# Stick-breaking rows by chunks from the last keys on, with only beta in a 4 KB slot

## The chip, the core and the metric

The kernel runs on one core of a Trainium2 chip. The core has a matrix engine (TensorE; in the profile PE for its matmuls and PEld for its weight loads), a vector engine (VectorE, DVE), an engine for functions such as the sigmoid (ScalarE, ACT), a general engine (GpSimd, POOL) and a queue that issues DMAs (SyncE, SP). Each takes its instructions strictly in the order that was fixed when the program was built, and stands when the next one has to wait for another engine. Operands lie in SBUF (128 partitions), matmul results in the banks of PSUM.

The metric is the device time of one execution in microseconds (us), lower being better. It is given as the median of several executions.

## What is computed

The reference is a trunk of two equal layers on 1024 tokens of width 1024. A combined projection of the stream feeds four parallel branches (latent attention "MLA", stick-breaking attention, forgetting attention "fox", attention to a memory of 256 tokens), each of 4 heads of width 64. The branches are gated and merged, projected, added to the stream and normalised. The branch that matters here:

```python
def _stick_breaking_attention(q, k, v):
    """A[t,s] = sigmoid(z[t,s]) * prod_{s<j<t} (1 - sigmoid(z[t,j])), s < t."""
    ...
    z = jnp.einsum('bqhd,bkhd->bhqk', qb, kb, preferred_element_type=jnp.float32)
    strict = jnp.arange(kend)[None, :] < (start + jnp.arange(Q_BLOCK))[:, None]
    log_keep = jnp.where(strict, jax.nn.log_sigmoid(-z), 0.0)
    ...
    a = jnp.where(strict, jnp.exp(z + incl), 0.0).astype(v.dtype)
    return jnp.einsum('bhqk,bkhd->bqhd', a, vb)
```

`incl` is the sum of `log_keep` from key s to the end of the row. So the weight of key s is beta(s) = sigmoid(z(s)), times the product of 1 - beta over all later keys that the query sees. Queries are taken in blocks of 128, and a block of queries sees the keys up to its own end.

## The kernel before

All matmuls run in a split form: an operand is held as a high and a low part, so a projection is three passes (lines 245 to 247). In each layer the branches follow one another: fox pair 0, fox pair 1, stick-breaking pair 0 and 1 (`run(units(sb[0], "sb"), ...)`, lines 840 and 845), then memory and MLA. A "pair" is two of the four heads.

A `Unit` is one head and two blocks of 128 queries ("rows" below). Its number `qg` from 0 to 3 tells how many keys its rows see: `qg` 3 has rows of 896 and 1024 keys, 2 of 640 and 768, 1 of 384 and 512, 0 of 128 and 256. The units of a head come in the order 3, 0, 2, 1 (`Q_ORDER`). Rows of more than 512 keys ("wide" rows, those of `qg` 2 and 3) take two chunks of scores, since a chunk fills one PSUM bank of 512 values: in both layers there are 64 stick-breaking rows, 32 of them wide.

`Unit.scores` (line 358) makes the rows of a unit. For stick-breaking, per chunk: two matmuls (lines 353 and 354) put the scores in a PSUM bank; ScalarE writes 1 - beta = sigmoid(-z) to `kt` and beta = sigmoid(z) to `bt` (lines 400 and 401, recorded under line 125, the helper `tfn`); at the row's last chunk POOL sets the masked part of the last 128 columns of `bt` to zero (line 403). After all chunks of the row:

```python
dve.tensor_tensor_scan(kt[:, ::-1], kt[:, ::-1], unseen[:, S - w:][:, ::-1], 1.0, ALU.mult, ALU.max)
dve.tensor_tensor(bt[:, :w - 1], bt[:, :w - 1], kt[:, 1:], ALU.mult)
```

The scan (line 416) runs from the last key back and leaves in `kt` the running product; its second operand `unseen` is 1 where the query doesn't see the key, which holds the product at 1 there. The product (line 417) takes for each key the running product of the key behind it.

`Unit.values` (line 433) then turns a row's `bt` by 128 x 128 transposes on TensorE into `pt` (line 442). `split_evac` (lines 143 to 149) copies it to `ph` on ScalarE (145) and takes the rest to `pl` on VectorE (146), and `product` (line 465) multiplies both with the values into `y` (line 472); `add_heads` (lines 460 and 461) adds up the halves. The products of a chunk are issued `LAG` = 2 chunks later.

`run` (line 510) interleaves: while the scores of one unit are made, the values of the unit `AHEAD` = 2 before it are worked through, and between the steps TensorE gets pieces of a "filler", the projections of the next pair (`pair_qkv`) or, in the second half, of `cq` and the merge input. The filler's weights come by DMA on the SP queue (line 221) and are split on POOL (lines 154 and 157); for `cq`, POOL also squares and sums (lines 749 to 753).

Storage: tiles of up to 512 float32 columns come from a pool of 64 slots of 2 KB per partition (`U`, pool `up`), wider ones from a pool of 7 slots of 4 KB (`W`, pool `wp`). Narrow rows take both `bt` and `kt` from the first pool, wide rows both from the second. A slot can be written again when the last reader of its tile is done; the framework adds the waits. It also fixes the order of the instructions on each engine: it goes by the order of the program and by when it reckons an instruction to be ready, so the order on an engine isn't just that of the text.

Of the kernel before, what the change touches and what calls it, by code (L numbers as in the profile page):

```python
# [10 lines left out]
F32 = mybir.dt.float32  # L11
F32R = mybir.dt.float32r
I32 = mybir.dt.int32
AF = mybir.ActivationFunctionType
ALU = mybir.AluOpType
# [6 lines left out]
S = 1024  # L22
# [15 lines left out]
HALF = 512  # L38
# [27 lines left out]
def decoder_trunk(ctx: ExitStack, tc: tile.TileContext, x, x_t, mem_t, positions, w_a, w_s, mla_q_norm, mla_w_qb,  # L66
# [3 lines left out]
    act, dve, pool, pe = nc.scalar, nc.vector, nc.gpsimd, nc.tensor  # L70
# [15 lines left out]
    def nm(s):  # L86
        uid[0] += 1
        return f"{s}_{uid[0]}"

    def U(s, dt=F32R):  # L90
        return up.tile([P, HALF], dt, tag="U", name=nm(s))

    def W(s, w=S):
        if w <= HALF:
            return U(s, F32)[:, :w]
        return wp.tile([P, S], F32, tag="W", name=nm(s))[:, :w]
# [4 lines left out]
    def SM(s, n=1):  # L101
        return sp.tile([P, 16], F32, tag="sm", name=nm(s))[:, :n]

    def PJ(s="pj"):
        return psj.tile([P, HALF], F32, tag="pj", name=nm(s))

    def PT(s="pt"):
        return pst.tile([P, HALF], F32, tag="pt", name=nm(s))

    def PS(s="sc"):  # L110
        return psj.tile([P, HALF], F32, tag="pj", name=nm(s))
# [8 lines left out]
    def after(later, earlier):  # L120
        tc.add_manual_dep(later.ins, earlier.ins.name,
                          mybir.DependencyInfo(mybir.DependencyClass.NoSync, mybir.DependencyReason.DATA), reason="table")

    def tfn(*args, **kw):
        i = act.activation(*args, **kw)  # L125
        if table_load[0] is not None:
            after(i, table_load[0])
        table_users.append(i)
# [39 lines left out]
    unseen = cp.tile([P, S], mybir.dt.bfloat16, name="unseen")  # L168
# [9 lines left out]
    ps = psy.tile([P, HALF], F32, tag="y", name="warm")  # L178
# [158 lines left out]
    class Unit:  # L337
# [20 lines left out]
        def scores(self):  # L358
            op, h = self.op, self.head
            if self.kind == "mem":  # L360
                ps = PS()
                for i in range(2):
                    self.qk(ps[:, i * MEM:(i + 1) * MEM], i, op["k"][h], 0, MEM)
                yield
                v3 = ps.rearrange("p (i k) -> p i k", i=2)
                mx = SM("mx", 2)
                dve.tensor_reduce(mx, v3, AX.X, ALU.max, negate=True)
                p = W("p", HALF)
                sm = SM("sm", 2)
                for i in range(2):  # L370
                    tfn(p[:, i * MEM:(i + 1) * MEM], ps[:, i * MEM:(i + 1) * MEM], AF.Exp,
                        bias=mx[:, i:i + 1], accum_out=sm[:, i:i + 1])
                dve.reciprocal(sm, sm)
                for i in range(2):
                    pool.tensor_scalar(p[:, i * MEM:(i + 1) * MEM], p[:, i * MEM:(i + 1) * MEM], sm[:, i:i + 1], 1.0,
                                       ALU.mult, ALU.mult)
                    self.p.append(p[:, i * MEM:(i + 1) * MEM])
                return
            for i in range(2):
                qb = 2 * self.qg + i  # L380
                w = (qb + 1) * P
                if self.kind == "sb":
                    bt, kt = W("bt", w), W("kt", w)
                else:
                    p = W("p", w)
                    bias = None
                    mx, sm = SM("mx", 2), SM("sm")
                if self.kind == "fox":
                    ckb, c_nat, hg = self.aux()
                    pool.tensor_scalar(p, ckb[:, :w], -1.0, c_nat[:, hg, qb:qb + 1], ALU.mult, ALU.add)  # L390
                    pool.affine_select(p[:, w - P:], p[:, w - P:], [[-1, P]], ALU.is_ge, -BIG, base=0, channel_multiplier=1)
                    bias = p
                for c0 in range(0, w, HALF):
                    n = min(HALF, w - c0)
                    ps = PS()[:, :n]
                    c = slice(c0, c0 + n)
                    self.qk(ps, i, op["k"][h][c0 // HALF][:, :n], c0, n)
                    yield
                    if self.kind == "sb":
                        tfn(kt[:, c], ps, AF.Sigmoid, scale=-1.0)  # L400
                        tfn(bt[:, c], ps, AF.Sigmoid)
                        if c0 + n == w:
                            pool.affine_select(bt[:, w - P:], bt[:, w - P:], [[-1, P]], ALU.is_gt, 0.0, base=0, channel_multiplier=1)  # L403
                    else:
                        if bias is not None:
                            b = bias[:, c]
                        elif c0 + n == w:
                            b = mask[:, HALF - n:]
                        else:
                            b = mask[:, 0:1].broadcast_to((P, n))  # L410
                        dve.tensor_tensor_reduce(out=p[:, c], in0=ps, in1=b, scale=-1.0,  # L411
                                                 scalar=mx[:, 0:1] if c0 else 3.0e38, op0=ALU.add, op1=ALU.min,
                                                 accum_out=mx[:, 1:2] if c0 else mx[:, 0:1])
                if self.kind == "sb":

                    dve.tensor_tensor_scan(kt[:, ::-1], kt[:, ::-1], unseen[:, S - w:][:, ::-1], 1.0, ALU.mult, ALU.max)
                    dve.tensor_tensor(bt[:, :w - 1], bt[:, :w - 1], kt[:, 1:], ALU.mult)
                    self.p.append(bt)
                    continue
                mx = mx[:, 1:2] if w > HALF else mx[:, 0:1]  # L420
                tfn(p, p, AF.Exp, bias=mx, scale=-1.0, accum_out=sm)
                dve.reciprocal(sm, sm)  # L422
                pool.tensor_scalar(p, p, sm, 1.0, ALU.mult, ALU.mult)  # L423
                self.p.append(p)
# [192 lines left out]
    for layer in range(DEPTH):  # L617
# [12 lines left out]
        for b in range(NB):  # L630
            if b == 4:
                drain(late_x.pop()())
            ps = PJ("pA")
# [25 lines left out]
        ps = PT("cum")  # L659
# [10 lines left out]
        ps = PT("cT")  # L670
# [53 lines left out]
        sb = [{}, {}]  # L724
# [469 lines left out]
        for col in range(2):  # L1194
# [5 lines left out]
            for t in range(NB):  # L1200
# [3 lines left out]
                ps = PJ("po")  # L1204
# [78 lines left out]
```

## Time and profile before

| | us |
|---|---|
| median of 3 runs | 1596.25 (1595.80 to 1597.51) |
| the profiled execution | 1594.06 |
| its span, first to last instruction | 1592.3 |
| mean granted TensorE clock | 0.998 |

The profile is of one execution, a little faster than the median of the others. Its span is shorter than the time of that execution by what lies before the first and after the last instruction. The groups of instructions that the change touches, by shape (engine, operation, out<-in, shapes, count; then busy time in all, mean duration in ns, and the idle time of the engine before them with what ended it):

```profile
L125 ACT ACTIVATE kt<-sc 128x512 f32<-128x512 f32 x48 | 29.4, 618 | 12.8 <-PE sc L354 12.6
L125 ACT ACTIVATE bt<-sc 128x512 f32<-128x512 f32 x48 | 29.1, 614 | 16.7 <-DVE bt L417 16.7
```

```profile
L416 DVE TENSOR_TENSOR_SCAN kt<-kt,unseen 128x896 f32<-128x896 f32 x8 | 18.3, 2291 | 0.1
L416 DVE TENSOR_TENSOR_SCAN kt<-kt,unseen 128x768 f32<-128x768 f32 x8 | 14.0, 1747 | 0.0
L417 DVE TENSOR_TENSOR bt<-bt,kt 128x895 f32<-128x895 f32 x8 | 9.6, 1194 | 0.0
L417 DVE TENSOR_TENSOR bt<-bt,kt 128x767 f32<-128x767 f32 x8 | 7.7, 967 | 0.5
```

A row of the first kind reads: 48 sigmoids of 128 x 512 take 29.4 us in all and 618 ns each, and ScalarE stood 12.8 us in front of them, 12.6 of which ended with a score matmul of line 354. In rows of a timeline the first number is the start, the second the duration. An engine that is idle costs nothing unless another one waits for it in the end.

### The profile page before, as it was taken

How to read it: one execution, taken by the hardware profiler on the slowest of the kernel's cores; microseconds unless marked ns; L12 is line 12 of the kernel's file. 1: busy time of each engine (PE TensorE's matmuls, PEld its weight loads, DVE VectorE, ACT ScalarE, POOL GpSimd, SP SyncE). 2: the span in 40 equal slices, each digit the busy share in tenths (PEclk: the TensorE clock that was granted, in tenths of full speed). 3: DMA queues.
4: the chain of work that ended last, by engine and by line, in shares of the span. 5: the costliest groups of instructions: out<-in, count | busy, mean ns of one | idle time of the engine just before them, and what ended most of it. 6: DMA issues, size and time to landing. Idle time of an engine off the chain costs nothing.

```text
span 1592.3 us, 24853 instructions
## 1 busy us (share of the span) xinstructions
PE 1559.3 (98%) x8454; PEld 1328.6 (83%) x8454; DVE 1027.2 (65%) x2047; ACT 737.7 (46%) x1628; POOL 810.3 (51%) x967
## 2 busy tenths in 40 slices
PE   9999999999999999999999999999999999999997
PEld 8888878888887888888898888788888878888886
DVE  6455588844417788882863566888444277888738
ACT  4354565534425666440423456565444256564301
POOL 5765535765544243671636654267645443446611
PEclk9999999999999999999999999999999999999999
DMA  5311112132233212252312221121422232212413
GB/s 183 113 57 54 52 35 64 54 121 59 80 108 106 70 38 60 79 172 80 116 61 87 60 62 50 30 64 58 122 61 77 101 110 70 64 39 81 149 47 119
DMA packets 86062, 127.93 MB, mean 80 GB/s; under 512 B 13424, under 2 KB 38832, under 8 KB 85936
## 3 DMA queue, kind: packets, MB, share of 16 engines
q1 hardware_dynamic: 85936, 126.34, 25.5%
q8 instruction: 67, 1.10, 0.3%
q14 instruction: 59, 0.48, 0.1%
HBM read 89.57 MB, written 19.96 MB: 69 GB/s over the span
## 4 chain that ended last, share of the span: by engine, by line
PE 83%; DVE 7%; POOL 3%; issue 3%; ACT 2%; DMA 2%; SPq 0%; DVEq 0%; ACTq 0%; POOLq 0%
PE pj L245 12%; PE pj L246 12%; PE pj L247 12%; PE y L472 6%; PE pt L442 6%; PE sc L353 3%; PE pb L245 3%; PE sc L354 3%; PE pb L246 3%; PE pb L247 3%; PE po L245 3%; PE po L247 3%; PE po L246 3%; PE pg L245 1%; PE pg L247 1%
## 5 line engine op out<-in xcount | busy, mean ns | idle before, releaser
L245 PE MATMUL pj<-xTh,wh 128*128 128x512 f32 x832 | 330.3, 397 | 0.0
L247 PE MATMUL pj<-xTh,wl 128*128 128x512 f32 x832 | 326.6, 392 | 0.0
L246 PE MATMUL pj<-xTl,wh 128*128 128x512 f32 x832 | 325.9, 392 | 0.0
L157 POOL TENSOR_TENSOR wl<-wr,wh 128x512 fp32r<-128x512 f32 x168 | 226.6, 1350 | 9.6
L154 POOL TENSOR_SCALAR wh<-wr 128x512 fp32r<-128x512 f32 x168 | 121.9, 726 | 212.9 <-PE pj L246 118.1
L146 DVE TENSOR_TENSOR pl<-pt,ph 128x384 fp32r<-128x384 f32 (+1 forms) x272 | 171.1, 637 | 90.9 <-ACT ph L145 89.0
L145 ACT CAST ph<-pt 128x384 fp32r<-128x384 f32 (+1 forms) x272 | 148.7, 552 | 141.2 <-PE pt L442 137.7
L247 PEld LDWEIGHTS pj<-xTh,wl 128*128 128x128 f32 x832 | 156.4, 188 | 31.3
L423 POOL TENSOR_SCALAR p<-p,sm 128x896 f32<-128x896 f32 (+7 forms) x128 | 102.4, 802 | 152.7 <-DVE sm L422 151.8
L245 PEld LDWEIGHTS pj<-xTh,wh 128*128 128x128 f32 x832 | 156.5, 188 | 26.6 <-DVE mx L411 1.2
L246 PEld LDWEIGHTS pj<-xTl,wh 128*128 128x128 f32 x832 | 156.5, 188 | 25.7
L125 ACT ACTIVATE p<-p,mx 128x896 f32<-128x896 f32 (+7 forms) x128 | 99.6, 778 | 65.0 <-DVE mx L411 56.3
L472 PE MATMUL y<-pl,v 128*128 128x256 f32 (+1 forms) x544 | 123.8, 305 | 0.0
L125 ACT ACTIVATE mg<-pg 128x512 f32<-128x512 f32 x128 | 76.4, 597 | 90.8 <-PE pg L247 54.4
L472 PE MATMUL y<-ph,v 128*128 128x256 f32 (+1 forms) x544 | 113.0, 285 | 0.2
L442 PE MATMUL pt<-ident_r,p 128*128 128x128 f32 x704 | 110.8, 273 | 1.5 <-DVE pl L146 1.4
L245 PE MATMUL pb<-ybh,wh 128*128 128x512 f32 x256 | 102.8, 402 | 4.7 <-ACT ybh L148 2.0
L472 PEld LDWEIGHTS y<-ph,v 128*128 128x128 f32 x544 | 92.8, 189 | 12.2 <-issue 0.9
L246 PE MATMUL pb<-ybl,wh 128*128 128x512 f32 x256 | 100.5, 392 | 0.1
L247 PE MATMUL pb<-ybh,wl 128*128 128x512 f32 x256 | 100.1, 391 | 0.0
L403 POOL TENSOR_SCALAR_AFFINE_SELECT bt<-bt 128x128 f32<-128x128 f32 x64 | 53.5, 841 | 90.4 <-ACT bt L125 85.4
L442 PEld LDWEIGHTS pt<-ident_r,p 128*128 128x128 f32 x704 | 84.7, 140 | 16.1 <-DVE pl L146 2.3
(277 smaller groups left out, 3626.6 us busy)
## 6 DMA issues: line engine op xcount, KB each, us to landing
wr<-in_w_s_dram SPq DMA_DIRECT2D x168, 256.0 KB, 2.6
s<-opA SPq DMA_DIRECT2D x128, 64.0 KB, 2.0
s<-opB SPq DMA_DIRECT2D x128, 64.0 KB, 2.0
wr<-in_w_out_dram SPq DMA_DIRECT2D x32, 256.0 KB, 2.6
xr<-in_x_t_dram SPq DMA_DIRECT2D x16, 256.0 KB, 5.6
ckb<-c_d SPq DMA_DIRECT2D x8, 512.0 KB, 4.3
y_d<-y SPq DMA_DIRECT2D x16, 256.0 KB, 2.2
y<-y_d SPq DMA_DIRECT2D x16, 256.0 KB, 3.5
```

Source lines behind the costliest of these rows:

```text
L125: i = act.activation(*args, **kw)
L145: act.copy(h, src)
L146: return dve.tensor_tensor(l, src, f(h), ALU.subtract)
L154: i = pool.tensor_scalar(h, src, 1.0, 1.0, ALU.mult, ALU.mult)
L157: pool.tensor_tensor(l, src, f(h), ALU.subtract)
L245: pe.matmul(ps, ah, bh, start=k == 0, stop=False)
L246: pe.matmul(ps, ah, bl, start=False, stop=False)
L247: pe.matmul(ps, al, bh, start=False, stop=k == nk - 1)
L403: pool.affine_select(bt[:, w - P:], bt[:, w - P:], [[-1, P]], ALU.is_gt, 0.0, base=0, channel_multiplier=1)
L423: pool.tensor_scalar(p, p, sm, 1.0, ALU.mult, ALU.mult)
L442: pe.transpose(pt[:, c:c + P], self.p[i][:, b * P:(b + 1) * P], ident)
L472: pe.matmul(u.y[:, q0 * P:256], u.op["v"][b][:, u.head, :], src[:, s * 256 + q0 * P:s * 256 + 256], start=j == 0 and n == 0, stop=j == n_c ...
```

## The change

Only the stick-breaking part of `Unit.scores` changes. A row's `kt` is no longer one tile of the row's width: each chunk has its own `kt` of at most 512 columns, from the 2 KB slots. The chunks of a row are made from the last keys to the first. The scan and the product come chunk by chunk, as soon as the chunk's sigmoids are issued. The second chunk's scan starts from `later`, the first column of the `kt` before it, and the last column of a chunk's `bt`, which needs the running product of the chunk behind it, is multiplied by `later` in an operation of its own. `bt` stays one tile of the row's width. Rows of one chunk have the same operations as before. The other kinds of units keep their order of chunks.

```diff
-                    bt, kt = W("bt", w), W("kt", w)
+                    bt, later = W("bt", w), None
...
-                for c0 in range(0, w, HALF):
+                starts = list(range(0, w, HALF))
+                for c0 in reversed(starts) if self.kind == "sb" else starts:
...
                     if self.kind == "sb":
-                        tfn(kt[:, c], ps, AF.Sigmoid, scale=-1.0)
+
+
+                        kt = U("kt", F32)[:, :n]
+                        tfn(kt, ps, AF.Sigmoid, scale=-1.0)
                         tfn(bt[:, c], ps, AF.Sigmoid)
                         if c0 + n == w:
                             pool.affine_select(bt[:, w - P:], bt[:, w - P:], [[-1, P]], ALU.is_gt, 0.0, base=0, channel_multiplier=1)
+                        dve.tensor_tensor_scan(kt[:, ::-1], kt[:, ::-1], unseen[:, S - w:][:, c][:, ::-1],
+                                               1.0 if later is None else later, ALU.mult, ALU.max)
+                        if later is not None:
+                            dve.tensor_tensor(bt[:, c0 + n - 1:c0 + n], bt[:, c0 + n - 1:c0 + n], later, ALU.mult)
+                        dve.tensor_tensor(bt[:, c0:c0 + n - 1], bt[:, c0:c0 + n - 1], kt[:, 1:], ALU.mult)
+                        later = kt[:, 0:1]
...
                 if self.kind == "sb":
-
-                    dve.tensor_tensor_scan(kt[:, ::-1], kt[:, ::-1], unseen[:, S - w:][:, ::-1], 1.0, ALU.mult, ALU.max)
-                    dve.tensor_tensor(bt[:, :w - 1], bt[:, :w - 1], kt[:, 1:], ALU.mult)
                     self.p.append(bt)
```

## The prediction

> **What bounds the kernel now.** I read the page first, then the busy time of each engine by stretch, then the waits inside the stick-breaking stretches, and last the instructions one by one at the places where TensorE stood.
>
> ```profile
> span 1592.3 us, 24853 instructions
> PE 1559.3 (98%) x8454; PEld 1328.6 (83%) x8454; DVE 1027.2 (65%) x2047; ACT 737.7 (46%) x1628; POOL 810.3 (51%) x967
> PE 83%; DVE 7%; POOL 3%; issue 3%; ACT 2%; DMA 2%; SPq 0%; DVEq 0%; ACTq 0%; POOLq 0%
> ```
>
> TensorE is busy for 98% of the span and is 83% of the chain that ended last. The change adds and removes no matmul, so it can only act on the 1592.3 - 1559.3 = 33.0 us in which PE stands, and it touches only the two stick-breaking stretches, at 184 to 330 us and again at 978 to 1122 us. The columns below are the stretch, its length, and the busy time of PE, PEld, DVE, ACT and POOL.
>
> ```profile
> core 0: us, PE busy (x) PEld busy (x) DVE busy (x) ACT busy (x) POOL busy (x), PEclk, DMA share, GB/s
> 80.00:184.00 104.00, 102.76 (x589) 88.32 (x589) 58.21 (x165) 55.83 (x121) 63.72 (x96) 1.00 0.19 55
> 184.00:260.00 76.00, 71.99 (x406) 61.07 (x406) 63.19 (x79) 44.96 (x105) 31.56 (x31) 1.00 0.14 41
> 260.00:330.00 70.00, 69.13 (x390) 59.57 (x389) 55.91 (x69) 39.29 (x86) 45.01 (x40) 1.00 0.24 76
> ```
>
> The forgetting-attention stretch (80 to 184 us) loses 1.2 us of PE. The stick-breaking one (184 to 330 us) loses 4.01 + 0.87 = 4.9 us, with VectorE busy for 119.1 of 146 us against 58.2 of 104. So the ceiling of the gain is 4.9 us a layer, 9.8 us in all, or 0.6%.
>
> Who waits for whom there (total, times, longest). The first row is of the whole span, the rest are of 180 to 332 us:
>
> ```profile
> ACT bt L125 <- DVE bt L417: 16.7, 8, 2.4
> ...
> PE sc L353 <- ACT bt L125: 2.8, 3, 2.0
> PE pt L442 <- DVE pl L146: 1.9, 3, 0.9
> ...
> DVE bt L417 <- POOL bt L403: 2.2, 3, 0.9
> ...
> ACT bt L125 <- DVE bt L417: 8.4, 4, 2.4
> ```
>
> The sigmoid that writes `bt` reads only PSUM, so nothing of its data comes from L417. It waits for storage: L417 is the last reader of an earlier row's `kt`, whose 4 KB slot the new `bt` takes. By the code, rows of two wide units are in flight (4 `bt`) while the next wide unit makes two more `bt` and two `kt`: 8 for 7 slots.
>
> This is the longest such place, in order of time (start, duration, engine; in brackets the idle time before and what ended it):
>
> ```profile
> 218.82 1.09 ACT L125 ACTIVATE kt<-sc 128x512 f32<-128x512 f32 x2
> ...
> 219.07 4.28 DVE L416 TENSOR_TENSOR_SCAN kt<-kt,unseen 128x896 f32<-128x896 f32 x2
> ...
> 221.97 0.58 ACT L145 CAST ph<-pt 128x512 fp32r<-128x512 f32 x1 [2.06 <-PE pt L442]
> ...
> 223.28 1.43 DVE L417 TENSOR_TENSOR bt<-bt,kt 128x895 f32<-128x895 f32 x1
> ...
> 224.74 0.69 DVE L146 TENSOR_TENSOR pl<-pt,ph 128x512 fp32r<-128x512 f32 x1
> 224.80 1.08 ACT L125 ACTIVATE bt<-sc 128x512 f32<-128x512 f32 x2 [2.25 <-DVE bt L417]
> 225.45 0.39 PE L353 MATMUL sc<-opB,opB 128*128 128x256 f32 x1 [2.01 <-ACT bt L125]
> ...
> 226.05 0.49 PE L472 MATMUL y<-pl,v 128*128 128x256 f32 x2
> ```
>
> ACT waits 2.25 us until the multiplication of the 896 row ends at 224.71. The score banks in PSUM stay full meanwhile, and PE waits 2.01 us for one. I call this place A; it stands once in each layer.
>
> **The change part by part.** *TensorE, ACT, DMA.* Each wide row keeps its two score chunks with the short one now first: same matmuls, same 192 sigmoids of the same sizes, no DMA added or moved past another (the SP queue's head loads and weight loads stay behind the same steps). Cost 0.
>
> *Slots.* `kt` leaves the 4 KB slots, so at most 6 of 7 are asked for and the 16.7 us of ACT waits go. Of PE's time this is worth 2.01 us at A. What is late next there is `pl`. Without its wait PE reaches the product at 226.05 - 2.01 = 224.04, and in the present VectorE order `pl` ends at 224.74 + 0.69 = 225.43: then 1.39 us of the wait would stay and 0.62 be gained. But `ph` is ready at 221.97 + 0.58 = 222.55, and `pl` comes late only because two whole scans (4.28 us) and a product stand ahead of it. In pieces of at most 512 no VectorE operation there is longer than the 1.22 us of the 512 scan below, so `pl` can start by 223.77, end by 224.46 and keep PE for 0.42. I take 2.01 - 0.42 = 1.6 us, since the planner orders by readiness; the ends are 0.62 and 2.01. The other three ACT waits of a layer cost PE at most 2.8 - 2.01 = 0.8 us; I take 0.
>
> Here a page of the Trainium skill speaks on both sides. "Perfetto Trace Analysis", section Optimizing Scalar/DVE Operations, says that grouping into larger operations helps throughput where the engine is saturated, and that breaking instructions up may let work end sooner where it is not saturated but makes bubbles elsewhere. By its first half A would gain 0.62 or less, by its second half 1.6; no run so far shows which holds.
>
> *VectorE pays* by one more scan, one more product and a one-column product for each of the 32 wide rows (columns: busy us, mean ns, idle before):
>
> ```profile
> L416 DVE TENSOR_TENSOR_SCAN kt<-kt,unseen 128x1024 f32<-128x1024 f32 x8 | 20.4, 2552 | 2.1 <-ACT kt L125 2.1
> ...
> L422 DVE RECIPROCAL sm<-sm 128x1 f32<-128x1 f32 x128 | 20.2, 159 | 32.3 <-ACT p L125 31.1
> ...
> L416 DVE TENSOR_TENSOR_SCAN kt<-kt,unseen 128x640 f32<-128x640 f32 x8 | 12.8, 1602 | 1.8 <-ACT kt L125 1.8
> L417 DVE TENSOR_TENSOR bt<-bt,kt 128x1023 f32<-128x1023 f32 x8 | 11.9, 1487 | 3.0 <-POOL bt L403 3.0
> ...
> L416 DVE TENSOR_TENSOR_SCAN kt<-kt,unseen 128x512 f32<-128x512 f32 x8 | 9.8, 1222 | 0.1
> ...
> L417 DVE TENSOR_TENSOR bt<-bt,kt 128x511 f32<-128x511 f32 x8 | 8.9, 1107 | 1.8 <-POOL bt L403 1.4
> L417 DVE TENSOR_TENSOR bt<-bt,kt 128x639 f32<-128x639 f32 x8 | 8.7, 1094 | 0.7
> ...
> L416 DVE TENSOR_TENSOR_SCAN kt<-kt,unseen 128x128 f32<-128x128 f32 x8 | 4.0, 504 | 0.1
> ...
> L417 DVE TENSOR_TENSOR bt<-bt,kt 128x127 f32<-128x127 f32 x8 | 2.7, 339 | 0.5
> ```
>
> A 1024 row: scans 2 x 1222 - 2552 = -108 ns, products 2 x 1107 - 1487 = +727 ns. A 640 row: 1222 + 504 - 1602 = +124 and 1107 + 339 - 1094 = +352 ns. The one-column product is not in this trace; the nearest row is the one-column reciprocal, 159 ns. So a wide row costs 0.64 to 0.78 us more; at 0.7 that is 22 us in all, 11 us a layer. What hides it:
>
> ```profile
> 198.70:228.40 29.70, 26.52 (x148) 22.32 (x147) 28.02 (x36) 18.48 (x40) 11.41 (x13) 1.00 0.16 49
> 228.40:233.10 4.70, 4.70 (x30) 4.11 (x29) 0.04 (x2) 0.60 (x2) 0.00 (x0) 1.00 0.06 16
> 233.10:260.00 26.90, 26.07 (x152) 22.07 (x151) 25.38 (x32) 18.27 (x44) 13.79 (x12) 1.00 0.12 35
> ```
>
> VectorE has no air around A (28.02 of 29.70). The four wide rows there add 2.8 us and then run into 4.70 us in which VectorE does nothing: covered. The next stretch has four wide rows again, 2.8 us, and only 1.5 us of air, so VectorE ends it 1.3 us later. Two units of rows stand between a row and its transposes, which should absorb that; I charge 0.3 us a layer, the ends being 0 and, if all eight rows reached PE, 5.6.
>
> *The added wait.* The masking on POOL (L403) now stands in front of the product of the last chunk, with the first chunk's scan and the next `pl` queued behind that product on VectorE, and PE behind `pl`. Before, a whole row's scan covered it and 3 of 32 rows of a layer still waited, 2.2 us. This is the second place where PE stands, B:
>
> ```profile
> 288.79 3.36 DVE L416 TENSOR_TENSOR_SCAN kt<-kt,unseen 128x1024 f32<-128x1024 f32 x1
> ...
> 289.96 3.02 POOL L752 TENSOR_TENSOR q<-cq 128x512 f32<-128x512 f32 x1
> ...
> 292.94 0.29 POOL L403 TENSOR_SCALAR_AFFINE_SELECT bt<-bt 128x128 f32<-128x128 f32 x1
> ...
> 293.26 2.29 DVE L417 TENSOR_TENSOR bt<-bt,kt 128x1023 f32<-128x1023 f32 x1 [0.67 <-POOL bt L403]
> 295.48 1.14 DVE L146 TENSOR_TENSOR pl<-pt,ph 128x384 fp32r<-128x384 f32 x2
> ...
> 296.08 0.66 PE L442 MATMUL pt<-ident_r,bt 128*128 128x128 f32 x4 [0.87 <-DVE pl L146]
> ```
>
> POOL's square ends 0.83 us after the scan that ran beside it, the mask comes behind it, the product behind the mask, `pl` behind the product, and PE waits 0.87 us. With scans of at most 1.22 us the square should end earlier and `pl` find an earlier turn: I take +0.6 us a layer. The ends are +0.87 and -1.5 (if behind the mask there stand a 512 scan, a one-column product and two 511 products, 1.22 + 0.16 + 2 x 1.11 = 3.6 us, in place of 2.29, and 0.2 of slack goes too). The Trainium skill, "SBUF — State Buffer", section Who interferes with whom, says that a VectorE operation with two SBUF inputs and a POOL operation that reads SBUF exclude each other for the whole instruction, whichever started first. By that rule half-length scans would shorten POOL's wait, but more VectorE instructions would mean more collisions. The sum needs neither.
>
> *Sum:* per layer 1.6 + 0.6 - 0.3 = 1.9 us, 3.8 us in all: 1594.06 to about 1590.3 in the profiled execution, whose span is 1592.3. The median of the three runs shown is 2.2 us above that execution, so 1596.25 - 3.8 = 1592.5. A measurement of this kernel tells about 0.2%, 3.2 us, from no change.
>
> **The rivals.**
>
> *The wait is only passed on.* `pl` keeps its turn behind the scans and products, A gives 0.62 us, B gives 0, the charge stays: 2 x (0.62 - 0.3) = 0.6 us, so 1595.6. For it: around A VectorE is busy 28.02 of 29.70 us, and work is only added. Against it: the pieces open more turns.
>
> *VectorE becomes the bound.* It decides from the point at which the added work of a stretch is more than the air behind it. The eight wide rows of 198.7 to 260 us then cost 8 x 0.7 = 5.6 us of PE a layer, less 1.6 of A: +8 us, 1604.3. For it: 25.38 of 26.90 us. Against it: 4.70 us of air after A, and the two units of lead.
>
> *The 2 KB slots run short.* By my count of the code about 60 of the 64 are held here (32 of them the split stream, then q, k, v of two pairs, finished outputs, narrow rows), and two wide rows at once ask for 4 more. If they are short, the ACT wait only changes its pool and PE's 2.8 us a layer stay or grow: with VectorE's charge doubled to 0.6 and B at -1.5, 2 x 2.1 = +4.2 us, 1600.5. Against it: `vT`, `v` and the new q and k find slots in this trace without a listed wait. This is also the case in which the change does not do what it says.
>
> **How the numbers follow.** Forecast 0.55, of which 0.44 is a gain over 0.2% and 0.11 one within it; passed on 0.24, all within 0.2%; VectorE bound 0.15 and slots 0.06, both slower. Faster 0.44, same 0.35, slower 0.21. Low end: all of A (2.01), of B (0.87) and the 0.8 of the other waits, with 0.9 us a layer of short waits besides, is 9.2 us, 1587. High end: the slots' case and part of VectorE's, 1602; beyond it are 0.05 below and 0.10 above.
>
> **What would show it.** Right: no ACT `bt` wait on a VectorE product; PE's wait at the 256 row after the wide unit falls from 2.01 to under 0.6; VectorE's busy time in the two stretches grows by some 22 us; `pl` starts within 1.3 us of `ph` there. Wrong: the same PE time reappearing as "pt" or "y" waiting for `pl` (passed on), VectorE stretches without air longer than now and PE losing over 4.9 us a layer (bound), or `kt` sigmoids waiting for TensorE or VectorE readers of other tiles (slots). A different order of instructions throughout would make the sum wrong as a whole.

## The result, and the profile after

| | before | after |
|---|---|---|
| median, us | 1596.32 | 1609.15 |
| runs, lowest to highest, us | 1595.80 to 1597.51 | 1605.72 to 1610.48 |
| ratio of the runs | | 1.0078, 95% interval 1.0062 to 1.0094 |
| profiled execution, us | 1594.06 | 1610.48 |
| its span, us | 1592.3 | 1608.8 |

The change makes the kernel 0.8% slower; the forecast was 0.2% faster, and the time lies above the range. The ratios, here and below, come from the single runs and are not the quotients of the medians shown; the two differ by up to 0.1%. The page of the kernel after (span, busy time of the engines, chain):

```profile
span 1608.8 us, 24966 instructions
...
PE 1565.7 (97%) x8454; PEld 1332.6 (83%) x8454; DVE 1053.3 (65%) x2143; ACT 739.9 (46%) x1628; POOL 788.0 (49%) x967
...
PE 87%; DVE 7%; ACT 2%; DMA 1%; issue 1%; POOL 1%; SPq 0%; DVEq 0%; ACTq 0%; POOLq 0%
```

TensorE runs the same 8454 matmuls. VectorE is busy for 26.1 us more. The chain gives VectorE 7% before and after, so it does not show where the time went. The stretches do (length, busy PE, PEld, DVE, ACT, POOL, granted clock):

```profile
80.00:184.00 104.00, 102.76 (x590) 88.36 (x589) 58.22 (x165) 55.90 (x122) 63.77 (x96) 1.00 0.19 55
184.00:260.00 76.00, 71.27 (x389) 60.06 (x388) 63.30 (x101) 42.11 (x96) 23.35 (x29) 0.96 0.14 39
260.00:330.00 70.00, 64.71 (x366) 55.01 (x365) 63.25 (x89) 38.87 (x86) 41.09 (x40) 1.00 0.18 55
...
228.40:233.10 4.70, 3.29 (x18) 2.48 (x16) 4.60 (x6) 0.00 (x0) 3.06 (x2) 1.00 0.17 38
```

Up to 184 us nothing has changed. In the stick-breaking stretch TensorE now stands 4.73 + 5.29 = 10.0 us, against 4.9 before, and from 184 to 330 us it starts 755 matmuls where before it started 796. The last row is the 4.70 us in which VectorE had been idle before: it is now busy for 4.60 of them. The second layer repeats it; these are the sums for its stretch (978 to 1122 us), first before, then after:

```profile
sum 144.00, PE 139.10 PEld 119.03 DVE 118.66 ACT 81.76 POOL 76.04; mean PE 69.55 PEld 59.51 DVE 59.33 ACT 40.88 POOL 38.02
```

```profile
sum 144.00, PE 133.76 PEld 113.54 DVE 124.44 ACT 80.86 POOL 62.18; mean PE 66.88 PEld 56.77 DVE 62.22 ACT 40.43 POOL 31.09
```

TensorE stands 10.2 us there, 4.9 before. What it waits for in the kernel after, 180 to 345 us (total, times, longest):

```profile
PE pt L449 <- DVE pl L146: 6.7, 6, 2.2
PE sc L353 <- DVE v L312: 1.7, 2, 0.8
PE sc L353 <- ACT bt L125: 0.5, 1, 0.5
```

The wait that the change was to remove is gone: `bt` cost TensorE 2.8 us, and costs 0.5. But the wait for `pl` has grown from 1.9 to 6.7 us in this layer, and to 7.2 in the other. The wait for `v` is new; it comes at 193 and 263 us, where the two pairs start. The groups of instructions show that the sigmoids no longer wait, and how long VectorE's pieces take (columns as before: count, busy us, mean ns, idle before):

```profile
L125 ACT ACTIVATE bt<-sc 128x512 f32<-128x512 f32 x48 | 29.3, 610 | 0.0
...
L408 DVE TENSOR_TENSOR_SCAN kt<-kt,kt,unseen 128x512 f32<-128x512 f32 x32 | 44.7, 1395 | 0.1
L412 DVE TENSOR_TENSOR bt<-bt,kt 128x511 f32<-128x511 f32 x48 | 44.3, 924 | 1.7 <-POOL bt L407 0.7
L408 DVE TENSOR_TENSOR_SCAN kt<-kt,unseen 128x512 f32<-128x512 f32 x16 | 23.3, 1459 | 0.1
L411 DVE TENSOR_TENSOR bt<-bt,kt 128x1 f32<-128x1 f32 x32 | 8.2, 257 | 0.0
```

ScalarE's 16.7 us in front of the `bt` sigmoids are 0.0. The 512 scan, at 1222 ns in its row before, takes 1395 to 1459 ns, and the one-column product 257 ns where I had taken 159. Half of these products take 136 ns or less; single ones take up to 1185.

Place B in order of time, the second of the places where TensorE stands:

```profile
296.47 1.53 DVE L412 TENSOR_TENSOR bt<-bt,kt 128x511 f32<-128x511 f32 x1
...
297.41 1.49 POOL L759 TENSOR_TENSOR q<-cq 128x512 f32<-128x512 f32 x1
...
297.93 2.06 DVE L408 TENSOR_TENSOR_SCAN kt<-kt,unseen 128x512 f32<-128x512 f32 x1
297.94 0.58 ACT L145 CAST ph<-pt 128x512 fp32r<-128x512 f32 x1 [2.08 <-PE pt L449]
...
298.98 2.06 POOL L760 TENSOR_TENSOR sq<-sq,q 128x512 f32<-128x512 f32 x1
...
299.90 0.53 DVE L146 TENSOR_TENSOR pl<-pt,ph 128x384 fp32r<-128x384 f32 x1
...
300.49 0.66 PE L449 MATMUL pt<-ident_r,bt 128*128 128x128 f32 x4 [2.17 <-DVE pl L146]
```

A piece of a scan, 2.06 us long beside POOL's two operations, is put in front of `pl`, though `ph` was ready at 298.52. TensorE waits 2.17 us, where it had waited 0.87. The shorter pieces didn't give `pl` an earlier turn.

A second difference lies at the start of the stretch, on ScalarE. Before, the first `kt` follows the sigmoid's table load at once:

```profile
182.79 1.28 ACT L136 ACT_TABLE_LOAD   x1
184.09 0.60 ACT L125 ACTIVATE kt<-sc 128x512 f32<-128x512 f32 x1
```

After:

```profile
182.65 1.28 ACT L136 ACT_TABLE_LOAD   x1
...
189.95 0.48 ACT L145 CAST ph<-pt 128x384 fp32r<-128x384 f32 x1 [5.04 <-PE pt L449]
...
190.58 0.65 ACT L310 CAST v<-vtp 128x256 fp32r<-128x256 f32 x2
...
192.13 0.65 ACT L310 CAST v<-vtp 128x256 fp32r<-128x256 f32 x2 [0.52 <-PE vtp L306]
192.67 0.51 ACT L125 ACTIVATE kt<-sc 128x384 f32<-128x384 f32 x1
```

The first `kt` sigmoid now comes at 192.67 us, 8.6 us later, behind the four `v` tiles of its own pair, which no data joins to it. As I read the program, a tile of the 2 KB pool is first written no earlier than the tiles of this pool that the program makes before it. `kt` of a wide row is now such a tile, and the pair's `v` is made ahead of it. Before, the first `kt` that had a 2 KB slot, that of the narrow row of 128 keys, stood right behind `v` as well:

```profile
197.31 0.65 ACT L310 CAST v<-vtp 128x256 fp32r<-128x256 f32 x2 [4.44 <-PE vtp L306]
197.84 0.30 ACT L125 ACTIVATE kt<-sc 128x128 f32<-128x128 f32 x1
```

### The profile page after: what moved, and what is told of

Its sections match the earlier page's. It is cut to its first block, busy times and chain, and to the rows that moved or that the text cites. A ratio compares the mean times of both kernels' runs of the same rounds, so it can differ in the third digit from the quotient of the medians.

```text
span 1608.8 us, 24966 instructions
## 1 busy us (share of the span) xinstructions
PE 1565.7 (97%) x8454; PEld 1332.6 (83%) x8454; DVE 1053.3 (65%) x2143; ACT 739.9 (46%) x1628; POOL 788.0 (49%) x967
## 4 chain that ended last, share of the span: by engine, by line
PE 87%; DVE 7%; ACT 2%; DMA 1%; issue 1%; POOL 1%; SPq 0%; DVEq 0%; ACTq 0%; POOLq 0%
PE pj L245 12%; PE pj L246 12%; PE pj L247 11%; PE y L479 7%; PE pt L449 6%; PE pb L245 4%; PE pb L246 4%; PE pb L247 4%; PE sc L353 3%; PE sc L354 3%; PE po L246 3%; PE po L247 3%; PE po L245 3%; DVE kt L408 2%; PE pg L245 2%; PE pg L247 2%
## 5 line engine op out<-in xcount | busy, mean ns | idle before, releaser
L479 PEld LDWEIGHTS y<-ph,v 128*128 128x128 f32 x544 | 94.0, 189 | 13.9 <-ACT ph L145 1.6
L407 POOL TENSOR_SCALAR_AFFINE_SELECT bt<-bt 128x128 f32<-128x128 f32 x64 | 36.0, 564 | 125.2 <-ACT bt L125 122.6
```

What stands on the lines that cost most here:

```text
L479: pe.matmul(u.y[:, q0 * P:256], u.op["v"][b][:, u.head, :], src[:, s * 256 + q0 * P:s * 256 + 256], start=j == 0 and n == 0, stop=j == n_c ...
```

## The experiments

Three parts of the change were in question, and each was tried alone, undone, or given room: the cut operations on VectorE, the 2 KB slots for `kt`, and the order of the chunks. All ratios are to the kernel before, run on the same chip, with 95% intervals.

**One more 4 KB slot, before otherwise unchanged.** This takes away the wait that the change was aimed at, and nothing else.

```diff
-    up = ctx.enter_context(tc.tile_pool(name="up", bufs=64))
-    wp = ctx.enter_context(tc.tile_pool(name="wp", bufs=7))
+    up = ctx.enter_context(tc.tile_pool(name="up", bufs=62))
+    wp = ctx.enter_context(tc.tile_pool(name="wp", bufs=8))
```

> Before, with 8 in place of 7 slots of 4 KB, and 62 in place of 64 of 2 KB to pay for it; nothing else. It takes the storage wait away alone. Theory P (the 2 KB pool's order is what costs) and theory V (VectorE's added operations cost): the 2.01 us wait of PE at place A goes, no ACT wait of bt on L417 is left, and the time falls by 2 to 6 us, to 1590 to 1594. If the wait was covered anyway: within 3 us of 1596. If 62 slots are too few: slower.

Measured: 1587.7 us against 1594.56, ratio 0.9953 (0.9940 to 0.9966). The `bt` group of this kernel:

```profile
L125 ACT ACTIVATE bt<-sc 128x512 f32<-128x512 f32 x48 | 29.7, 618 | 0.0
```

and its waits of TensorE for the same stretch:

```profile
PE pt L442 <- DVE pl L146: 1.2, 2, 0.7
...
PE sc L353 <- ACT bt L125: 0.4, 1, 0.4
```

So the wait was a wait for a slot, as argued, and without it `pl` is not late either: 1.2 us against 1.9. It is worth 6.9 us, more than I had expected and twice the 3.2 that I gave place A. The two 2 KB slots it takes cost nothing, which a control shows:

```diff
-    up = ctx.enter_context(tc.tile_pool(name="up", bufs=64))
+    up = ctx.enter_context(tc.tile_pool(name="up", bufs=62))
```

> Before, with 62 in place of 64 slots of 2 KB; the control of the run with 8 slots of 4 KB. If the 2 KB pool has two slots to spare: within 3 us of before. If not: slower, and the run with 8 slots has to be read against this one.

Measured: 1595.13 against 1595.33, 1.0001 (0.9992 to 1.0011).

**The cut operations alone.** Before, with scan, one-column product and product cut in two at the end of the row; scores in the old order, `kt` in its 4 KB slot.

```diff
-                    dve.tensor_tensor_scan(kt[:, ::-1], kt[:, ::-1], unseen[:, S - w:][:, ::-1], 1.0, ALU.mult, ALU.max)
-                    dve.tensor_tensor(bt[:, :w - 1], bt[:, :w - 1], kt[:, 1:], ALU.mult)
+                    later = None
+                    for c0 in reversed(range(0, w, HALF)):
+                        n = min(HALF, w - c0)
+                        c = slice(c0, c0 + n)
+                        dve.tensor_tensor_scan(kt[:, c][:, ::-1], kt[:, c][:, ::-1], unseen[:, S - w:][:, c][:, ::-1],
+                                               1.0 if later is None else later, ALU.mult, ALU.max)
+                        if later is not None:
+                            dve.tensor_tensor(bt[:, c0 + n - 1:c0 + n], bt[:, c0 + n - 1:c0 + n], later, ALU.mult)
+                        dve.tensor_tensor(bt[:, c0:c0 + n - 1], bt[:, c0:c0 + n - 1], kt[:, c][:, 1:], ALU.mult)
+                        later = kt[:, c0:c0 + 1]
```

> Before, with the scan and the product of a wide row cut into chunks as in the changed kernel, but with kt still in a 4 KB slot, the scores in the old order, and both cut operations after the whole row. Theory V (VectorE's added operations make the loss): VectorE busy some 20 us more, and most of the loss is here, 1604 to 1610. Theory P (order of the 2 KB pool) and theory R (the reversed order of chunks): within 4 us of before, 1593 to 1600.

Measured: 1604.97, 1.0059 (1.0047 to 1.0072). Cutting alone costs 9.4 us of the 1594.56, though in this kernel mostly not by way of `pl`. TensorE's longest wait, once in each layer, is for a row's own last operations (line 423 is the one-column product there); for `pl` it waits 1.3 us, not more than before:

```profile
PE pt L450 <- DVE bt L423: 4.3, 1, 4.3
```

**The order alone.** Before, with only the chunks reversed.

```diff
-                for c0 in range(0, w, HALF):
+                starts = list(range(0, w, HALF))
+                for c0 in reversed(starts) if self.kind == "sb" else starts:
```

> Before, with only the order of the two score chunks of a wide row reversed; whole scans, kt in a 4 KB slot. Theory R (the order makes the loss, since the planner then orders everything else differently): 1603 to 1610. Theories P and V: within 4 us of before.

Measured: 1589.55, 0.9961 (0.9948 to 0.9974). The reversal is no harm, but a gain, which was not expected. The `bt` group says where from:

```profile
L125 ACT ACTIVATE bt<-sc 128x512 f32<-128x512 f32 x48 | 29.2, 613 | 5.4 <-DVE bt L418 5.4
```

16.7 us of waiting for a slot have become 5.4 with the same 7 slots. If this is the same wait as the first experiment's, the two gains should not add up. The reversal above, and one more slot:

```diff
-    up = ctx.enter_context(tc.tile_pool(name="up", bufs=64))
-    wp = ctx.enter_context(tc.tile_pool(name="wp", bufs=7))
+    up = ctx.enter_context(tc.tile_pool(name="up", bufs=62))
+    wp = ctx.enter_context(tc.tile_pool(name="wp", bufs=8))
```

> Before, with the reversed order of chunks and 8 slots of 4 KB (62 of 2 KB), whole scans. If the two gains are the same wait removed in two ways: 1586 to 1590, as with either alone. If they are of different waits: 1580 to 1585.

Measured: 1588.38 against 1595.4, 0.9953 (0.9936 to 0.9970): no more than the slot alone.

**The change with `kt` back in a 4 KB slot.**

```diff
-                    bt, later = W("bt", w), None
+                    bt, kw, later = W("bt", w), W("kt", w), None
...
-                        kt = U("kt", F32)[:, :n]
+                        kt = kw[:, c]
```

> The changed kernel in everything but storage: kt of a wide row is one tile in a 4 KB slot again, whose chunks are scanned one by one in the new order. Theory P: the first sigmoids come at about 184 us again in place of 192.7, and most of the loss goes, 1594 to 1602. Theory V or R: the loss stays, 1606 to 1612.

Measured: 1597.89, 1.0016 (1.0007 to 1.0025). This is the reversal's kernel plus the cuts: 0.9961 to 1.0016, so here they cost 0.55%. And it is 0.6% faster than the whole change, so the place of `kt` costs too. With eight 4 KB slots as well, no shortage is left, and only the operations differ from the kernel with reversed order and eight slots. The edit above, and:

```diff
-    up = ctx.enter_context(tc.tile_pool(name="up", bufs=64))
-    wp = ctx.enter_context(tc.tile_pool(name="wp", bufs=7))
+    up = ctx.enter_context(tc.tile_pool(name="up", bufs=62))
+    wp = ctx.enter_context(tc.tile_pool(name="wp", bufs=8))
```

> The changed kernel with kt of wide rows in 4 KB slots of which there are 8 (62 of 2 KB): order, cut operations and enough slots, without the 2 KB pool. Theory V (the cut operations cost by themselves): 6 to 12 us above the run that has the reversed order and whole scans, 1593 to 1599. If the cut operations cost only because slots run short: within 3 us of that run.

Measured: 1600.61 against 1595.4, 1.0032 (1.0021 to 1.0043). Against its twin without cuts that is 12.2 us. The same stretch of time in both, first without cuts, then with them:

```profile
280.00:300.00 20.00, 20.00 (x115) 17.27 (x114) 16.91 (x19) 9.70 (x22) 15.79 (x14) 1.00 0.21 60
```

```profile
280.00:300.00 20.00, 17.77 (x92) 15.42 (x91) 18.05 (x20) 8.10 (x17) 13.03 (x11) 0.91 0.19 53
```

and inside them, with cuts, in order of time:

```profile
288.49 2.31 DVE L408 TENSOR_TENSOR_SCAN kt<-kt,unseen 128x512 f32<-128x512 f32 x1
...
290.73 3.00 DVE L412 TENSOR_TENSOR bt<-bt,kt 128x383 f32<-128x383 f32 x2
...
293.75 1.16 DVE L146 TENSOR_TENSOR pl<-pt,ph 128x512 fp32r<-128x512 f32 x2
...
294.50 0.90 PE L449 MATMUL pt<-ident_r,bt 128*128 128x128 f32 x3 [2.23 <-DVE pl L146]
```

A scan and two products, 5.3 us, run in front of `pl`. With whole operations TensorE does not stand there at all.

**Which of the cuts.** The reversed kernel with eight slots, with the scan cut, chunk by chunk, and the product left whole.

```diff
+                        dve.tensor_tensor_scan(kt[:, ::-1], kt[:, ::-1], unseen[:, S - w:][:, c][:, ::-1],
+                                               1.0 if later is None else later, ALU.mult, ALU.max)
+                        later = kt[:, 0:1]
...
-                    dve.tensor_tensor_scan(kt[:, ::-1], kt[:, ::-1], unseen[:, S - w:][:, ::-1], 1.0, ALU.mult, ALU.max)
-                    dve.tensor_tensor(bt[:, :w - 1], bt[:, :w - 1], kt[:, 1:], ALU.mult)
+                    dve.tensor_tensor(bt[:, :w - 1], bt[:, :w - 1], kw[:, 1:], ALU.mult)
```

> Reversed order, 8 slots of 4 KB, the scan cut by chunks as they come, but the product whole, at the row's end: one more operation for each wide row in place of three. With whole operations this is 1588, with all three 1600.6. Theory V by time (what counts is VectorE's busy time, some 5 of the 18 us): 1589 to 1593. Theory V by number (each further operation is a turn more for pl to wait for): 1591 to 1597, a third of the way. If cutting the scan is what costs: 1598 to 1602.

Measured: 1597.95 against 1595.7, 1.0013 (1.0004 to 1.0022). From 0.9953 that is 0.60%, 9.6 us, of the 0.79% that all the cuts cost: the scan's cut, which I had priced at about nothing, makes most of the loss. One row of each kernel, first the whole scans, then the cut ones:

```profile
L417 DVE TENSOR_TENSOR_SCAN kt<-kt,unseen 128x1024 f32<-128x1024 f32 x8 | 20.8, 2604 | 2.1 <-ACT kt L125 2.1
```

```profile
L408 DVE TENSOR_TENSOR_SCAN kt<-kt,unseen 128x512 f32<-128x512 f32 x48 | 69.0, 1442 | 2.4 <-ACT kt L125 1.1
```

Two halves take 2 x 1442 = 2884 ns instead of 2604. Over all widths the scans take 110.5 us instead of 96.6. Of these 48 pieces, 23 have no POOL operation on tensors beside them and take 1.27 us on average; the other 25 take 1.61 us. Among those 25, the 12 that run beside an operation of POOL on two tensors (`TENSOR_TENSOR`) take 1.92 us, the other 13 take 1.32.

**The turn in the pool.** First, the change with a pool of its own for the wide rows' `kt`: three 2 KB slots, taken from the common ones.

```diff
-    up = ctx.enter_context(tc.tile_pool(name="up", bufs=64))
+    up = ctx.enter_context(tc.tile_pool(name="up", bufs=61))
+    kp = ctx.enter_context(tc.tile_pool(name="kp", bufs=3))
...
-                        kt = U("kt", F32)[:, :n]
+                        kt = (kp.tile([P, HALF], F32, tag="K", name=nm("kt")) if w > HALF else U("kt", F32))[:, :n]
```

> The changed kernel, with the kt chunks of wide rows in a pool of their own, 3 slots of 2 KB that the common pool gives up (61 in place of 64). Theory P (a tile of the common 2 KB pool gets its slot in the order of the program, behind tiles of the filler): the first sigmoids come at about 184 us again, and most of the loss goes, 1592 to 1602. Theory V (VectorE's added operations): the loss stays, 1606 to 1612.

Measured: 1606.55 against 1595.33, 1.0067 (1.0053 to 1.0081), which is what theory V had said. The first `kt` was back at 183.8 us, but time was lost outside the stick-breaking stretches too: its matmuls fall some 4 us behind those of before between 553 and 603 us, and again between 1334 and 1386. So a control was needed: the kernel before with 61.

```diff
-    up = ctx.enter_context(tc.tile_pool(name="up", bufs=64))
+    up = ctx.enter_context(tc.tile_pool(name="up", bufs=61))
```

> Before, with 61 in place of 64 slots of 2 KB: the control of the run with a pool of its own for kt. That run lost its time outside of the stick-breaking stretches, by its trace some 9 us. If the lack of three slots does it: 1602 to 1608. If not: within 3 us of before.

Measured: 1603.34 against 1595.4, 1.0048 (1.0029 to 1.0067). Taking it off leaves 1.0067 / 1.0048 = 1.0019 for the own pool, if the two losses simply add; with both intervals that is anything from 0.9995 to 1.0043.

Second, with no slot taken: the change, but the `kt` of the first unit of the first pair in a 4 KB slot.

```diff
-                    bt, later = W("bt", w), None
+                    bt, kw, later = W("bt", w), (W("kt", w) if self.first else None), None
...
-                        kt = U("kt", F32)[:, :n]
+                        kt = U("kt", F32)[:, :n] if kw is None else kw[:, c]
...
-        run(units(sb[0], "sb"), pair_qkv(sb[1], SC64), 49)
+        sb_units = units(sb[0], "sb")
+        sb_units[0].first = True
+        run(sb_units, pair_qkv(sb[1], SC64), 49)
```

> The changed kernel, with kt of only the first unit of each layer's stick-breaking (two rows of 32 kt chunks) in a 4 KB slot. Theory P (a kt of the 2 KB pool gets its slot only after the values' tiles that stand ahead of it in the program): ScalarE's first sigmoid moves from 192.7 back to 184 us, the 3.4 us of PE waits of the first 6 us go in each layer, with the halved clock behind them, and the time falls by 6 to 11 us, to 1598 to 1603. If the loss of the storage step is spread over all rows: within 3 us of the changed kernel, 1606 to 1612.

Measured: 1607.82, 1.0074 (1.0058 to 1.0091): nothing, where I had expected most of the turn's cost back. The trace showed why the experiment was too small. The first `kt` came at 183.8 us, but the second pair's first one was as late as in the change, behind the next `v` tiles there too. ScalarE there, in the change:

```profile
261.84 0.65 ACT L310 CAST v<-vtp 128x256 fp32r<-128x256 f32 x2 [1.89 <-PE vtp L306]
262.37 0.51 ACT L125 ACTIVATE kt<-sc 128x384 f32<-128x384 f32 x1
```

So the same was done for both pairs. The edit above, and:

```diff
-        run(units(sb[1], "sb"), chain(cq_proj(), proj(evac_mr)), 58)
+        sb_units = units(sb[1], "sb")
+        sb_units[0].first = True
+        run(sb_units, chain(cq_proj(), proj(evac_mr)), 58)
```

> The changed kernel, with kt in a 4 KB slot for the first unit of both stick-breaking pairs of a layer (4 rows of 32 in all), in the 2 KB pool for the rest. With the first pair's alone, ScalarE's sigmoids of the second pair's first unit still came at 262 us, where they come at 246 to 253 us with all kt in 4 KB slots; the values' tiles of the next pair stand ahead of them in the 2 KB pool there too. Theory P (the turn in the 2 KB pool): these sigmoids move back to 246 to 253 us, the waits of PE at 261 to 271 us go, and the time comes to that of the version with all kt in 4 KB slots, 1597 to 1602. If the turn only moves the waits: 1604 to 1609.

Measured: 1601.27 against 1595.7, 1.0034 (1.0022 to 1.0047). In its trace:

```profile
249.60 0.49 ACT L125 ACTIVATE kt<-sc 128x384 f32<-128x384 f32 x1
```

The second pair's first `kt` comes at 249.60 instead of 262.37 us. From 1.0078 to 1.0034 is 0.44%, 7 us, for the turns of two units in each layer (eight of the 32 wide rows); all other `kt` stay in the 2 KB pool. TensorE's wait for `pl` did not shrink with it: 14.2 us over the span, 13.9 in the change. So this is a term beside that of VectorE.

**Together:**

| term | from | ratio | us of 1596 |
|---|---|---|---|
| no wait for a 4 KB slot | one more slot, or the order | 0.9953 | -7.5 |
| scans and products cut | three pairs of kernels: 0.55, 0.59 and 0.79% | + 0.0079 | +12.6 |
| first `kt` of each pair late | 1.0078 against 1.0034 | + 0.0044 | +7.0 |
| sum | | 1.0076 | +12.1 |
| measured | | 1.0078 | +12.5 |

The sum takes the cut's price from the pair without a shortage of slots. The terms' own intervals are some 0.2% wide or more, so the agreement is closer than they warrant. The cuts also do not cost at the same places in every kernel: made in the old order they add TensorE's standing between 184 and 260 us (8.0 us against 4.0), in the pair used here mostly between 260 and 330 us (3.2 against 0.0). Each term holds TensorE's standing and what its clock lost behind it (last section). Of the kernels run, the one with an eighth 4 KB slot, paid for with two of 2 KB, is the fastest (with the reversed order it is the same): 0.9953 of before, and 1.2% less than the change.

## Why the prediction was wrong

*What bounds the kernel: right.* Only the stick-breaking stretches moved, and TensorE's standing there carries the difference.

*"At most 6 of 7 are asked for and the 16.7 us of ACT waits go": right, and mis-sized.* They go. I gave A 1.6 us a layer, since `pl` would be late next there, and the other three places 0; an added slot gives 3.5 us a layer. My ceiling of 4.9 us of standing was fair, but I took the gain of one place for the gain of the stretch.

*"VectorE pays ... I charge 0.3 us a layer, the ends being 0 and ... 5.6": this is the step that failed.* The cuts cost 4.4 to 6.3 us a layer (0.55 to 0.79%), around the upper end and over it. The amount of work was nearly right: 22 us forecast, 26.1 measured. Its parts were not. From the rows for lines 416 and 417 of before, taken over all shapes, to those of after, the scans grew by 12.0 us (93.3 to 105.3), where -108 to +124 ns a row had meant about nothing; the products grew by 11.0 (59.9 to 70.9), where 32 rows at +352 to +727 ns had meant some 17; and the one-column product added 8.2 where 32 at 159 ns are 5.1. That is 31.2 us; VectorE's other work took 5.1 us less. I had read the 512 scan's cost from eight scans, none of which had a two-tensor operation of POOL beside it. In the kernel after, 11 of the 48 have one and take 1.92 us; the other 37 take 1.27. The rule that I had cited from the Trainium skill, "SBUF — State Buffer", section Who interferes with whom, is that a VectorE operation with two SBUF inputs contends with a POOL operation that reads SBUF. The 1.27 and 1.92 us agree with it, and here it is VectorE that pays. I had used the rule for POOL's wait alone and said that the sum needed no more.

*"Covered" was the larger error.* I compared 2.8 us of added work with 4.70 us of idle time behind A and trusted two units of lead for the rest. The idle time filled (4.60 of 4.70 us), and TensorE stood for `pl` all the same. For that wait, what counts is what stands in front of one `pl` on VectorE, not whether the stretch has room in the end. The two units of lead did not hold either where the cuts were made in the old order: there TensorE waited 4.3 us for a row itself. And I had looked at only eight of a layer's sixteen wide rows, those from 198.7 to 260 us. Two lie before and six behind, where TensorE stood 5.29 us between 260 and 330 us instead of 0.87. That is most of what was added, though the late `kt` of the second pair falls there too. The rival "VectorE becomes the bound" had the mechanism and a price of 5.6 us a layer, at a chance of 0.15; its 1604.3 was still below the 1609.15.

*Place B, "`pl` find an earlier turn", +0.6 us: fell.* It went to the other end that I had named: the wait there rose by 2.17 - 0.87 = 1.3 us, within the bound of 1.5. That the bound held is partly luck: I had four operations behind the mask in mind, and it was one scan, made long by POOL. The same belief in more turns for shorter pieces had carried the 1.6 us at A. Of the two halves of the rule that I had cited from the Trainium skill ("Perfetto Trace Analysis", section Optimizing Scalar/DVE Operations) the first held: in a stretch where VectorE is full (16.91 of 20 us in the rows from 280 us), the larger operations were the better ones, 0.9953 against 1.0032.

*"Same 192 sigmoids of the same sizes ... Cost 0": failed as well.* Their sizes are the same, but their place on ScalarE is not: the first `kt` of a pair came 8.6 us later in the first pair. The rival that I tied to the 2 KB pool, a shortage of slots, is not what happened: the sign that I had named for it, `kt` waiting for readers of other tiles, is not what delays the first `kt` at 192.67 us, which follows its `v` tiles without idle time. Two later `kt` wait 1.3 us in all over the span for line 411, and could be of that kind. I had looked at the pool's size and not at the order in which it gives out its slots. No case of mine had this term. The upper bound of 1602 allowed for part of VectorE's case, and the 7 us here come on top of it. The forecast has no term for TensorE's clock either; in the profiled execution that is 6.4 of the 16.5 us (last section).

*Open.* Eight slots do not make the cut version faster than seven (1.0032 against 1.0016, 2.6 us), though they do without cuts. The granted clock is lower with eight, 0.9960 on average against 0.9976. In the kernel after, 0.004 of clock went with 4.8 us, so this would be some 2 of the 2.6 us, but why it is lower there is not shown. How the reversed order spares the slot wait is not shown beyond the row with 5.4 us. That the late `kt` follows from the pool's order is read from the program's order and from the two kernels that bypass it; a pool of its own with no common slot lost was not tried.

## What to carry to other kernels

Where an engine waits for storage, add a slot or change the order in which the slots are asked for before cutting operations on an engine that is already full: here the slot alone gave -0.5% and the cuts took it back and more. Price an added operation by what it puts in front of the next short operation on which TensorE waits, not by the idle time of the stretch around it. A tile moved to a shared pool can also come to take a turn there, behind tiles that the program makes earlier, so look at what is made before it.

## What was not expected of the hardware

The granted clock of TensorE fell to half for single stretches of 3.41 us, right behind stretches in which it had stood for much of the time. Windows of the kernel after:

```profile
190.00:197.32 7.32, 5.21 (x35) 4.14 (x33) 6.13 (x11) 6.58 (x16) 1.70 (x2) 1.00 0.07 19
197.32:200.73 3.41, 3.17 (x8) 2.52 (x9) 3.32 (x6) 2.72 (x8) 0.89 (x2) 0.50 0.16 41
231.00:234.86 3.86, 2.18 (x14) 1.42 (x14) 3.86 (x7) 0.94 (x2) 0.54 (x1) 1.00 0.23 71
234.87:238.27 3.40, 3.40 (x13) 2.82 (x12) 3.22 (x7) 2.55 (x8) 0.59 (x2) 0.50 0.00 0
```

The first and third rows are what came ahead, with TensorE busy for 71% and 56%; then it ran 3.4 us at clock 0.50, each time worth some 1.7 us. This happened four times in this execution. Over the whole of it TensorE's busy time grew by 6.4 us (1559.3 to 1565.7) with the same matmuls, and its standing by 10.1; together these are the 16.5 us by which the span grew.

It is not the same in every run. The kernel after took 1610.48 us at a mean clock of 0.994 and 1605.72 at 0.998, which is still 11.7 us more than the 1594.06 of before at that clock. The profile of before has no such stretch before its last microseconds, nor have those of the kernel with one more slot and of the one with both first units in 4 KB slots, which is still slower than before. The control with 62 slots has two in its profiled execution, which took 1597.81 us, 2.7 above its own median.

Other kernels with cut operations pay in this way too, and the ratios do not tell it apart. The one with only the scan cut ran at 0.994 to 0.996 in all of its eleven executions, its twin with whole operations at 0.997 to 0.999 in all six. Between their profiled executions the span grew by 10.2 us (1586.0 to 1596.2), of which 5.2 are TensorE's busy time (1558.0 to 1563.2) and 5.0 its standing. So about half of what the cut costs there is clock.

"TensorE: Matmul & The Clock Gate" of the Trainium skill, in the section on what is actually happening, gives free-running windows of 3413 ns, which the rows fit, and says that the clock falls after at least one idle window. Here it fell without such a window: in the 3.41 us right ahead of the four stretches TensorE was busy for 2.13, 1.73, 2.03 and 1.40 us, and ahead of the two shown here it stood for no longer than 1.51 us at a time. Which share decides, these runs don't show.
